# A decoder layer on one core: weights and remainders stored alternately, and requests moved in the front

## The chip, the cores and the metric

The kernel runs on one core of a Trainium2 chip. The core has TensorE (PE) for matmuls, VectorE (DVE), ScalarE (ACT) and GpSimd (POOL) for the rest, and SyncE (SP), which here issues nearly all transfers. The metric is the device time of one execution in microseconds (us); the timed runs of a kernel are compared by their median.

## The reference

One decoder layer for 256 tokens of width 1024, all in float32. Cut to what matters:

```
h = rmsnorm(x, norm_mix_g);  q, k, v, gu, gv, gate_a, gate_b = split(h @ w_in)
y_a = moba_attention(rope(q), rope(k), v) @ moba_w_proj        # 8 heads, one causal block of 256
y_b = gmlp_spatial_gating(gu, gv, ...) @ gmlp_w_proj
x = x + (sigmoid(gate_a) * y_a + sigmoid(gate_b) * y_b) @ w_out
x = x + memory_cross_attention(rmsnorm(x), rmsnorm(mem), xa_w_q, xa_w_kv, xa_w_o)
# PEER: 128 x 128 experts of one neuron, 8 heads, top 16
q = rmsnorm(x) @ peer_w_q;  s = q . subkeys                    # two scores per head and token
top 16 of s1, top 16 of s2, top 16 of their 256 sums -> experts e, g = softmax(top scores)
x = x + sum_k g_k * gelu(h . w_down[e_k]) * w_up[e_k]
return rmsnorm(x, final_g)
```

The kernel doesn't gather experts. It computes all 16384 of `h . w_down` (128 down blocks of 128 experts), multiplies by a gate that is zero where an expert wasn't chosen, and multiplies by all of `w_up` (128 up blocks).

## The kernel before

**Weights as a stream.** All weights lie in HBM as blocks of 128 x 1024 float32 (512 KB): 84 of the front (`wf`), 128 down (`wd`), 128 up (`wu`). `load_to` requests a block into one of four `raw` buffers on SP. `conv_to` splits it in two: ACT writes `hi`, the block rounded to fp32r (L140), and DVE the remainder `lw` = raw - hi (L142; for the routing's query blocks and the first five down blocks POOL does it). `take` hands a block to PE and first converts two blocks ahead (`LEAD`) and requests four more (`RAW`). Functions that were put into `later` run inside `take`, after that. Each product is then three fp32r matmuls: hi by hi, hi by remainder, remainder by hi (`mm3`, L179 to L181).

**Two kinds of blocks.** In most blocks the weights are the stationary operand: PE loads 128 columns of `hi` or `lw` and streams 256 columns of activations past them, 24 matmuls a block (`tblock` in the front, `down` for the experts, tile `A`). In 12 front blocks (`Natural`, indices 0 to 3, 12 to 15, 48, 49, 62, 63 of `wf`) and all up blocks (`umm`, tile `y`) the weights stream, 512 columns a matmul, past stationary activations: 12 matmuls a block. For up blocks the stationary operand is the gated activation, split into halves `gh` and `gl` in the tile `gahl`.

**Where the halves lie.** `hi` and `lw` are two tiles of three buffers each, every row contiguous. Small tiles `apart` and `rest` set their start 64 bytes behind a multiple of 512 (`APART`), and `GOFF` does the same for `gahl`.

**Order.** One program order, written out by hand; each engine runs its own instructions in it. Ahead: the first norm, q and k blocks with `rope`, attention, gates, gMLP, the memory's blocks, the output projection (`mp` by eight blocks, residual `x1T`, L606), cross-attention (`xquery`, `xscore`, `xscale`, `xtrans`, `xvalue`, with two value blocks `nm_.step()` among them), its projection, and 16 query blocks of the routing with the top-16 search of each (`best`) on DVE. Four remainders (`spread`) are already done in two halves of 512 there, popped from the list `half` at chosen places.

Then DVE merges the candidates (`work`, a list of pieces with an estimate of each), and `down` blocks are set beside it: `D0` = 22, one for each 1.55 us of estimate, and `D1` = 4 more while the last routing steps run. After them come 16 gate steps for the first 64 experts of each block (`gprep` on DVE makes one-hot fp16 patterns, `gstep` multiplies them on PE and ACT copies the result to `G`), then 64 up blocks, then 16 gate steps and 64 up blocks for the second half. `plan()` spreads the rest of the down blocks: a ring of 49 results (`RING`) bounds how many may be ahead, so the first gate stage has 49 - (D0 + D1 + 1) = 22 of them, the up stage 42, the second gate stage 22, the rest 15.

Of the kernel before, what the change touches and what calls it, by code (L numbers as in the profile page):

```python
# [16 lines left out]
F32 = mybir.dt.float32  # L17
# [10 lines left out]
S = 256  # L28
KD = 8
# [9 lines left out]
APART = 64  # L39
GOFF = (64, 64)  # L40
D0, D1 = 22, 4
# [4 lines left out]
N_XO, N_PQ = 4, 16  # L46
FIRST = 5
# [42 lines left out]
def body(tc, I, out, dbg=None):  # L90
# [18 lines left out]
    spread, half = range(nf - N_PQ - 2, nf - N_PQ + 2), []  # L109
    pos = {"load": 0, "conv": 0, "take": 0}  # L110

# [17 lines left out]
    def conv_to(n):  # L129
        while pos["conv"] < min(n, len(stream)):  # L130
            m = pos["conv"]
            load_to(m + 1)
            raw = raws.pop(m)
            hi = wst.tile([128, 1024], F32R, name="hi")
            lw = wst.tile([128, 1024], F32R, name="lw")
            parts = 2 if m in (1, 2) else 1
            halves = m in spread
            for p in range(parts):
                ps = slice(p * 1024 // parts, (p + 1) * 1024 // parts)
                A.copy(hi[:, ps], raw[:, ps])  # L140
                if not halves:
                    lo_engine(m).tensor_sub(lw[:, ps], raw[:, ps], hi[:, ps].bitcast(F32))  # L142
            if halves:
                for p in range(2):
                    ps = slice(p * 512, p * 512 + 512)
                    half.append(lambda ps=ps, lw=lw, raw=raw, hi=hi: V.tensor_sub(lw[:, ps], raw[:, ps],
                                                                                 hi[:, ps].bitcast(F32)))
            convs[m] = (hi, lw)
            pos["conv"] += 1
# [77 lines left out]
    P.dma_start(gcol, I["gcol"])  # L227
# [24 lines left out]
    class Squares:  # L252
# [5 lines left out]
        def add(self, src, sq=P, add=P):  # L258
            q = self.pool.tile([128, S], F32, name="sq", bufs=4)
            if sq is A:  # L260
                A.activation(q, src, AF.Square)
            else:
                sq.tensor_mul(q, src, src)
            if self.acc is None:
                self.acc = q
            else:
                add.tensor_add(q, q, self.acc)  # L267
                self.acc = q
# [20 lines left out]
    def tblock(w, x, n=KD, base=0):  # L289
        ps = pmm()  # L290
        for k in range(n):
            c = (base + k) * 128
            mm3(ps, w, (slice(None), slice(c, c + 128)), x, sl(k), k == 0, k == n - 1)
        return ps

    class Natural:
# [5 lines left out]
        def step(self):  # L302
            wh, wl = take("f")
# [17 lines left out]
    hi = wst.tile([128, 1024], F32R, name="hi")  # L321
    lw = wst.tile([128, 1024], F32R, name="lw")
# [23 lines left out]
    sqp.matmul()  # L346
# [6 lines left out]
    later.append(first_norm)  # L353
# [24 lines left out]
    for c in range(4):  # L378
        for nm in ("q", "k"):
            ps = tblock(take("f"), xg)  # L380
            if (c, nm) == (0, "q"):
                later.append(rope_norm)
# [221 lines left out]
    for c in range(KD):  # L604
        ps = tblock(take("f"), mp)
        V.tensor_add(x1T[:, c], ps, xT[:, c])  # L606
        split(xg1[0][:, c], xg1[1][:, c], x1T[:, c], gcol[:, 1, c:c + 1])
        pq.add(x1T[:, c], A, V)
    dump("x1T", x1T)
# [65 lines left out]
    xscale(1)  # L675
    xscore(3)
    xscale(2)
    nm_.step()
    xscale(3)
# [3 lines left out]
    P.dma_start(skh[0], I["skT"][:, 0:8])  # L683
    nm_.step()
    V.tensor_scalar(vm[:, 0], nm_.ps[0], rm[:, 0:1], None, op0=OP.mult)
    A.activation(vm[:, 1], nm_.ps[1], AF.Copy, scale=rm[:, 1:2])
    xtrans(0, 2)
# [63 lines left out]
    for n in range(16):  # L751
# [17 lines left out]
        if n == 7:  # L769
# [106 lines left out]
    for (us, fn) in work:  # L876
        fn()
        spent += us
        while n < D0 and spent > 1.55 * (n + 1) - 2.5:
# [115 lines left out]
    def up_b(i2):  # L995
        if i2 in GA:
            ga = GA.pop(i2)
            off = GOFF[i2 // QI] // 4
            gg_ = gp.tile([128, 2 * S + 128], F32R, name="gahl", bufs=4)
            gh, gl = gg_[:, off:off + S], gg_[:, off + S:off + 2 * S]  # L1000
# [169 lines left out]
```

## Time and profile before

| what | us |
|---|---|
| median of three timed runs (1053.73 to 1054.83) | 1054.41 |
| profiled execution, its own time | 1054.2 |
| its span, first to last instruction | 1052.2 |
| PE busy in the span | 1031.1 (98%) |
| DVE busy | 763.3 (73%) |
| ACT busy | 594.0 (56%) |
| POOL busy | 64.1 (6%) |

Times in rows are microseconds from the start of the span unless marked ns. A row of PE's timeline gives a matmul's start and its length in the pipeline; lengths overlap, so the pace is read from start to start. "PEld" are weight loads. A busy PE is not a PE at its peak.

### The profile page before, as it was taken

Reading aid. Unit: us, or ns where it says so; the run is one execution under the profiler, and the core shown is the slowest. Engines: PE = TensorE matmul, PEld = TensorE weight load, DVE = VectorE, ACT = ScalarE, POOL = GpSimd, SP = SyncE. Lnnn points to the kernel's source line nnn. Section 1 sums busy time; section 2 is a strip of 40 time slices with the busy share of each in tenths; the row PEclk is TensorE's granted clock in tenths of the full one; section 3 lists DMA queues with packets and bytes.
Section 4 is the critical chain, followed back from the end, with each engine's and each line's share of the span. In section 5 each row is a group of like instructions: output and inputs, shape, how many; then the busy total and the mean of one; then the engine's idle time right before and its main releaser. Section 6 shows DMA issues by size and latency. Waiting matters only on the chain.

```text
span 1052.2 us, 19738 instructions
## 1 busy us (share of the span) xinstructions
PE 1031.1 (98%) x7862; PEld 954.5 (91%) x7862; DVE 763.3 (73%) x1493; ACT 594.0 (56%) x935; POOL 64.1 (6%) x54
## 2 busy tenths in 40 slices
PE   8999999889999999999999999999999999999997
PEld 7989999889999999998889988999999988888886
DVE  6775797579999999965656565566799766666656
ACT  6865845457554557755454444444678644545454
POOL 0400000006650000000000000000000000000000
PEclk9999999899999999999999999999999999999999
DMA  8644655445446544465556655565544556566562
GB/s 283 235 138 128 200 170 174 134 152 170 151 158 202 166 140 152 134 187 189 192 187 194 191 190 189 191 195 188 160 147 154 176 189 196 187 195 191 191 197 103
DMA packets 52251, 185.83 MB, mean 177 GB/s; under 512 B 5808, under 2 KB 6720, under 8 KB 52032
## 3 DMA queue, kind: packets, MB, share of 16 engines
q1 hardware_dynamic: 51552, 183.20, 54.5%
q8 instruction: 61, 1.00, 0.4%
q0 software_dynamic: 320, 1.07, 0.3%
q10 hardware_dynamic: 288, 0.33, 0.1%
q14 instruction: 30, 0.25, 0.1%
HBM read 183.52 MB, written 1.05 MB: 175 GB/s over the span
## 4 chain that ended last, share of the span: by engine, by line
PE 85%; DVE 10%; ACT 3%; issue 1%; DMA 1%; SPq 0%; DVEq 0%; ACTq 0%
PE A L179 11%; PE y L1010 11%; PE y L1013 11%; PE y L1009 11%; PE A L181 11%; PE A L180 11%; PE mm L179 4%; PE mm L180 4%; PE mm L181 4%; DVE lw L142 2%; PE m L982 2%; ACT hi L140 2%; PE m L981 2%; DVE sq L267 1%; DVE X L727 1%
## 5 line engine op out<-in xcount | busy, mean ns | idle before, releaser
L142 DVE TENSOR_TENSOR lw<-raw,hi 128x1024 fp32r<-128x1024 f32 (+1 forms) x318 | 388.4, 1223 | 235.2 <-ACT hi L140 234.6
L140 ACT CAST hi<-raw 128x1024 fp32r<-128x1024 f32 (+1 forms) x341 | 355.2, 1043 | 191.0 <-issue 145.2
L179 PE MATMUL A<-mgh,hi 128*128 128x256 f32 x1024 | 290.6, 284 | 0.0
L181 PE MATMUL A<-mgh,lw 128*128 128x256 f32 x1024 | 288.0, 281 | 1.8 <-DVE lw L142 1.8
L180 PE MATMUL A<-mgl,hi 128*128 128x256 f32 x1024 | 287.8, 281 | 0.0
L181 PEld LDWEIGHTS A<-mgh,lw 128*128 128x128 f32 x1024 | 195.9, 191 | 2.2 <-DVE lw L142 2.2
L1010 PE MATMUL y<-lw,gahl 128*128 128x512 f32 x504 | 196.3, 390 | 0.0
L1009 PE MATMUL y<-hi,gahl 128*128 128x512 f32 x504 | 196.2, 389 | 0.0
L180 PEld LDWEIGHTS A<-mgl,hi 128*128 128x128 f32 x1024 | 192.9, 188 | 2.2
L179 PEld LDWEIGHTS A<-mgh,hi 128*128 128x128 f32 x1024 | 192.4, 188 | 2.2
L1013 PE MATMUL y<-hi,gahl 128*128 128x512 f32 x504 | 155.3, 389 | 0.0
L797 ACT ACTIVATE aring<-A 128x256 f32<-128x256 f32 x128 | 49.2, 384 | 161.4 <-PE A L181 161.4
L179 PE MATMUL mm<-xgh,hi 128*128 128x256 f32 x416 | 118.5, 285 | 0.2 <-DVE q L368 0.2
L181 PE MATMUL mm<-xgh,lw 128*128 128x256 f32 x416 | 116.2, 279 | 0.4 <-DVE lw L142 0.4
L180 PE MATMUL mm<-xgl,hi 128*128 128x256 f32 x416 | 116.0, 279 | 0.0
L1013 PEld LDWEIGHTS y<-hi,gahl 128*128 128x128 f32 x504 | 94.6, 188 | 19.6
L1010 PEld LDWEIGHTS y<-lw,gahl 128*128 128x128 f32 x504 | 94.7, 188 | 17.3
L1009 PEld LDWEIGHTS y<-hi,gahl 128*128 128x128 f32 x504 | 94.6, 188 | 17.4
L179 PEld LDWEIGHTS mm<-xgh,hi 128*128 128x128 f32 x416 | 78.3, 188 | 1.1 <-issue 0.7
L181 PEld LDWEIGHTS mm<-xgh,lw 128*128 128x128 f32 x416 | 78.6, 189 | 0.7 <-DVE lw L142 0.6
L180 PEld LDWEIGHTS mm<-xgl,hi 128*128 128x128 f32 x416 | 78.5, 189 | 0.0
L983 ACT ACTIVATE G<-m 128x512 f32<-128x512 f32 x64 | 65.9, 1140 | 5.0 <-PE m L982 2.3
(273 smaller groups left out, 1243.7 us busy)
## 6 DMA issues: line engine op xcount, KB each, us to landing
raw<-in_wd SPq DMA_DIRECT2D x128, 512.0 KB, 3.7
raw<-in_wu SPq DMA_DIRECT2D x128, 512.0 KB, 3.8
raw<-in_wf SPq DMA_DIRECT2D x83, 512.0 KB, 3.7
memT<-in_memT SPq DMA_DIRECT2D x1, 1024.0 KB, 7.8
xT<-in_xT SPq DMA_DIRECT2D x3, 256.0 KB, 7.0
out_y<-raw SPq DMA_DIRECT2D x3, 256.0 KB, 2.0
raw<-in_wf SPq DMA_DIRECT2D x2, 256.0 KB, 3.7
wmT<-in_wsT SPq DMA_DIRECT2D x1, 512.0 KB, 5.9
```

Source lines behind the costliest of these rows:

```text
L140: A.copy(hi[:, ps], raw[:, ps])
L142: lo_engine(m).tensor_sub(lw[:, ps], raw[:, ps], hi[:, ps].bitcast(F32))
L179: T.matmul(ps, wh[wsl], xh[xsl], start=start, stop=False)
L180: T.matmul(ps, wh[wsl], xl[xsl], start=False, stop=False)
L181: T.matmul(ps, wl[wsl], xh[xsl], start=False, stop=stop)
L797: A.activation(a, ps, AF.Gelu_apprx_tanh)
L981: T.matmul(ps[:, t], a1[at], bh[at], start=True, stop=False)
L982: T.matmul(ps[:, t], a1[at], bl[at], start=False, stop=True)
L983: A.activation(Gq[q][:, :, s * TG + c:s * TG + c + 8].rearrange("p i t -> p t i"), ps, AF.Copy, scale=1.0 / 16384.0)
L1009: T.matmul(yps[t][z], gh[:, tsl(t)], wh[:, zs], start=False, stop=False, skip_group_check=True)
L1010: T.matmul(yps[t][z], gh[:, tsl(t)], wl[:, zs], start=False, stop=False, skip_group_check=True)
L1013: T.matmul(yps[t][z], gl[:, tsl(t)], wh[:, zs], start=False, stop=False, skip_group_check=True)
```

## The change

Seven edits, in one diff (line numbers of the later kernel are some 15 higher from the top on):

- `hi` and `lw` become one tile `hl` of 2048. For blocks whose weights stream (`streamed`) its first half is `hi` and its second `lw` (`planar`); for all others, element by element, one of `hi` and one of `lw` (`woven`). `gahl` is woven too, without the offset, and `APART` is 128.
- `D0` is 26 and the pieces' pace 1.31 for 1.55. `plan()` then gives the first gate stage 49 - 31 = 18 down blocks, the up stage 46, the second gate stage 18, the rest 15.
- the mean square's matmuls move into the middle of the first q block, the broadcast of the norm into the middle of the first k block (`mid`); the norm itself is computed right behind the q block; `sq` has six buffers.
- the request of `gcol` goes from POOL to ACT.
- nine more remainders (`spread`) are done in halves: those of eight blocks in the output projection's loop and one behind `vm`.
- a value block goes ahead of `xscore(3)`, and `xscale(3)` behind a request.
- the third norm's broadcast goes one query block later.

```diff
-APART = 64
-GOFF = (64, 64)
-D0, D1 = 22, 4
+APART = 128
+D0, D1 = 26, 4
+NATURAL = [0, 1, 2, 3, 12, 13, 14, 15, 48, 49, 62, 63]
-    spread, half = range(nf - N_PQ - 2, nf - N_PQ + 2), []
+    spread, half = [*range(52, 60), nf - N_PQ - 3, *range(nf - N_PQ - 2, nf - N_PQ + 2)], []
+    def woven(x):
+        x = x.rearrange("p (c u) -> p c u", u=2)
+        return x[:, :, 0], x[:, :, 1]
+    def planar(x):
+        n = x.shape[1] // 2
+        return x[:, :n], x[:, n:]
+    def streamed(m):
+        kind, idx = stream[m]
+        return kind == "u" or kind == "f" and idx in NATURAL
-            hi = wst.tile([128, 1024], F32R, name="hi")
-            lw = wst.tile([128, 1024], F32R, name="lw")
+            hl = wst.tile([128, 2048], F32R, name="hl")
+            hi, lw = planar(hl) if streamed(m) else woven(hl)
-    P.dma_start(gcol, I["gcol"])
+    A.dma_start(gcol, I["gcol"])
-            q = self.pool.tile([128, S], F32, name="sq", bufs=4)
+            q = self.pool.tile([128, S], F32, name="sq", bufs=6)
-    def tblock(w, x, n=KD, base=0):
+    def tblock(w, x, n=KD, base=0, mid=None):
         ps = pmm()
         for k in range(n):
+            if mid and k == n // 2:
+                mid()
...
     nv.step()
-    sqp.matmul()
...
-            ps = tblock(take("f"), xg)
-            if (c, nm) == (0, "q"):
-                later.append(rope_norm)
+            first = c == 0
+            ps = tblock(take("f"), xg, mid=(sqp.matmul if nm == "q" else rope_norm) if first else None)
+            if first and nm == "q":
+                first_norm()
...
         V.tensor_add(x1T[:, c], ps, xT[:, c])
+        half.pop(0)()
         split(xg1[0][:, c], xg1[1][:, c], x1T[:, c], gcol[:, 1, c:c + 1])
         pq.add(x1T[:, c], A, V)
+        half.pop(0)()
...
     xscale(1)
+    nm_.step()
     xscore(3)
     xscale(2)
-    nm_.step()
-    xscale(3)
     xtrans(0, 0)
     xtrans(1, 0)
...
+    xscale(3)
     nm_.step()
     V.tensor_scalar(vm[:, 0], nm_.ps[0], rm[:, 0:1], None, op0=OP.mult)
     A.activation(vm[:, 1], nm_.ps[1], AF.Copy, scale=rm[:, 1:2])
+    for _ in range(2):
+        half.pop(0)()
...
-        if n == 7:
+        if n == 8:
             bcast(r3, r3bc)
...
-        while n < D0 and spent > 1.55 * (n + 1) - 2.5:
+        while n < D0 and spent > 1.31 * (n + 1) - 2.5:
...
-            off = GOFF[i2 // QI] // 4
-            gg_ = gp.tile([128, 2 * S + 128], F32R, name="gahl", bufs=4)
-            gh, gl = gg_[:, off:off + S], gg_[:, off + S:off + 2 * S]
+            gh, gl = woven(gp.tile([128, 2 * S], F32R, name="gahl", bufs=4))
```

On DVE, at the end of the output projection's loop, the order before is this (`lw` the remainder of a block two ahead, `xT` the residual sum, `xg1l` the remainder of the next operand, `sq` the squares' sum):

```order
L142 TENSOR_TENSOR lw<-raw,hi 128x1024
L606 TENSOR_TENSOR xT<-mm,xT 128x256
L175 SCALAR_TENSOR_TENSOR xg1l<-xT,gcol,xg1h 128x256
L267 TENSOR_TENSOR sq<-sq 128x256
L142 TENSOR_TENSOR lw<-raw,hi 128x1024 x2
```

And of the change, at the same place (`hl<-raw,hl` is a half of a remainder; the last row are the whole ones of the next two blocks):

```order
L621 TENSOR_TENSOR xT<-mm,xT 128x256
L160 TENSOR_TENSOR hl<-raw,hl 128x512
L189 SCALAR_TENSOR_TENSOR xg1l<-xT,gcol,xg1h 128x256
L281 TENSOR_TENSOR sq<-sq 128x256
L160 TENSOR_TENSOR hl<-raw,hl 128x512
L156 TENSOR_TENSOR hl<-raw,hl 128x1024 x2
```

The residual sum of a block now stands ahead of a remainder, and the remainder is cut in two around the next operand's split.

On DVE in cross-attention, before (`Px` the softmax's numerators, `xr` a reciprocal, `PT` a copy of transposes, `vm` the memory's values):

```order
L142 TENSOR_TENSOR lw<-raw,hi 128x1024
L649 RECIPROCAL xr<-xs 128x2
L651 TENSOR_SCALAR Px_2414<-Px_2414,xr 128x256
L651 TENSOR_SCALAR Px_2415<-Px_2415,xr 128x256
L641 COPY PT<-at 128x512
L142 TENSOR_TENSOR lw<-raw,hi 128x1024
L685 TENSOR_SCALAR vm<-nat_1749,rrr 128x512
```

Of the change:

```order
L658 COPY PT<-at 128x512
L666 RECIPROCAL xr<-xs 128x2
L668 TENSOR_SCALAR Px_2362<-Px_2362,xr 128x256
L668 TENSOR_SCALAR Px_2363<-Px_2363,xr 128x256
L702 TENSOR_SCALAR vm<-nat_1707,rrr 128x512
L160 TENSOR_TENSOR hl<-raw,hl 128x512 x2
```

The remainder that stood ahead of `vm` stands behind it, in halves.

On PE, at the end of the fourth query block, before (`at<-kT,qT` the scores of two heads, `nat` a value block):

```order
L181 MATMUL mm<-xg1h,lw 128x256
L625 MATMUL at<-kT,qT 128x256 x4
L310 MATMUL nat_1749<-hi,mgh 128x512
L311 MATMUL nat_1749<-lw,mgh 128x512
L312 MATMUL nat_1749<-hi,mgl 128x512
```

Of the change, from the last matmul of the value block on (the third head's two stand ahead of its 12 matmuls):

```order
L329 MATMUL nat_1708<-hl,mgl 128x512
L642 MATMUL at<-kT,qT 128x256 x2
L655 MATMUL at<-ident,Px_2362 128x128 x4
L655 MATMUL at<-ident,Px_2363 128x128 x4
L327 MATMUL nat_1707<-hl,mgh 128x512
```

The value block lies between the scores of the third and the fourth head, where the two stood in a row.

## Rows read from the trace of the kernel before

**Rows 1.** Part 4 of the page: the chain that ended last, by engine.

```profile
PE 85%; DVE 10%; ACT 3%; issue 1%; DMA 1%; SPq 0%; DVEq 0%; ACTq 0%
```

**Rows 2.** Stages: length, each engine's busy us (instructions), granted clock, DMA share, GB/s.

```profile
192.00:204.00 12.00, 9.67 (x52) 9.23 (x52) 7.41 (x17) 5.04 (x10) 0.00 (x0) 0.72 0.56 171
238.00:293.70 55.70, 53.99 (x461) 53.60 (x460) 53.26 (x260) 35.06 (x69) 38.81 (x16) 1.00 0.50 161
293.70:374.40 80.70, 78.56 (x666) 77.91 (x664) 77.33 (x313) 40.08 (x59) 11.08 (x14) 1.00 0.55 178
374.40:453.80 79.40, 79.36 (x1042) 78.34 (x1042) 71.93 (x85) 59.63 (x75) 0.00 (x0) 1.00 0.44 140
453.80:746.70 292.90, 292.90 (x1779) 263.02 (x1779) 176.37 (x238) 142.37 (x213) 0.00 (x0) 1.00 0.60 191
746.70:829.00 82.30, 82.27 (x1066) 81.22 (x1065) 74.17 (x89) 62.54 (x80) 0.00 (x0) 1.00 0.46 145
829.00:1045.00 216.00, 216.00 (x1127) 186.20 (x1126) 138.10 (x210) 107.85 (x164) 0.00 (x0) 1.00 0.58 184
```

**Rows 3.** Timeline of PE, 102 to 105 us: start, length, line, operation, tiles.

```profile
102.50 0.28 PE L179 MATMUL mm<-xgh,hi 128*128 128x256 f32 x1
...
105.22 0.28 PE L179 MATMUL mm<-xgh,hi 128*128 128x256 f32 x1
```

**Rows 4.** Timeline of PE, 699 to 705 us.

```profile
699.68 0.28 PE L179 MATMUL A<-mgh,hi 128*128 128x256 f32 x1
...
702.51 0.39 PE L1009 MATMUL y<-hi,gahl 128*128 128x512 f32 x1
...
705.23 0.28 PE L179 MATMUL A<-mgh,hi 128*128 128x256 f32 x1
```

**Rows 5.** Timeline of PE, 377 to 378 us: one gate step.

```profile
377.20 0.20 PE L981 MATMUL m<-bh,a 128*128 128x64 f16 x1
...
378.19 0.36 PE L179 MATMUL A<-mgh,hi 128*128 128x256 f32 x1
```

**Rows 6.** Timeline of PE ahead of 224 us; in brackets the wait before.

```profile
20.66 0.61 PE L273 MATMUL at<-ones,sq 128*128 128x1 f32 x4 [0.98 <-DVE sq L267]
...
169.01 0.28 PE L179 MATMUL mm<-xgh,hi 128*128 128x256 f32 x1
...
196.66 0.39 PE L179 MATMUL mm<-xg1h,hi 128*128 128x256 f32 x1 [1.82 <-ACT xg1h L170]
...
204.48 0.47 PE L179 MATMUL mm<-xg1h,hi 128*128 128x256 f32 x1
...
213.88 1.13 PE L625 MATMUL at<-kT,qT 128*128 128x256 f32 x4 [1.76 <-ACT qT L620]
...
223.81 1.38 PE L658 MATMUL mm<-PT,vm 128*128 128x128 f32 x10 [1.52 <-DVE vm L685]
```

**Rows 7.** Timeline of DVE and ACT, 194 to 196 us.

```profile
194.51 1.23 DVE L142 TENSOR_TENSOR lw<-raw,hi 128x1024 fp32r<-128x1024 f32 x1 [0.42 <-ACT hi L140]
...
195.65 0.42 DVE L606 TENSOR_TENSOR xT<-mm,xT 128x256 f32<-128x256 f32 x1
...
196.10 0.51 ACT L170 ACTIVATE xg1h<-xT,gcol 128x256 fp32r<-128x256 f32 x1 [1.63 <-DVE xT L606]
```

**Rows 8.** Groups of DVE by form: line, count, busy us, mean ns.

```profile
L142 DVE TENSOR_TENSOR lw<-raw,hi 128x1024 fp32r<-128x1024 f32 x314 | 385.9, 1230 | 234.7 <-ACT hi L140 234.1
...
L146 DVE TENSOR_TENSOR lw<-raw,hi 128x512 fp32r<-128x512 f32 x8 | 5.5, 686 | 0.4
```

**Rows 9.** Groups of ACT by form.

```profile
L983 ACT ACTIVATE G<-m 128x512 f32<-128x512 f32 x64 | 65.9, 1140 | 5.0 <-PE m L982 2.3
...
L643 ACT COPY PT<-at 128x512 f32<-128x512 f32 x2 | 1.2, 582 | 0.0
```

**Rows 10.** Groups of DVE by form, 328 to 361 us.

```profile
L844 DVE SCALAR_TENSOR_TENSOR jk<-XP,CE 128x48 f32<-128x48 f32 x4 | 0.8, 211 | 0.0
...
L844 DVE SCALAR_TENSOR_TENSOR jk<-XP,CE 128x32 f32<-128x32 f32 x4 | 0.8, 201 | 0.0
```

More of the change, by code (lines that the diff above doesn't have):

```diff
@@ L302, in step @@
         def step(self):
+            assert streamed(pos["take"])
             wh, wl = take("f")
@@ L320, in body @@
     wst.tile([128, APART // 4], F32, name="apart", bufs=1)
-    hi = wst.tile([128, 1024], F32R, name="hi")
-    lw = wst.tile([128, 1024], F32R, name="lw")
+    hi, lw = planar(wst.tile([128, 2048], F32R, name="hl"))
     wst.tile([128, 128 - APART // 4], F32, name="rest", bufs=1)
@@ L351, in first_norm @@
         r1 = rms_nat(sqp, fp, "r1")
-    later.append(first_norm)
     rbc = fp.tile([128, S], F32, name="rbc")
```

## Prediction

> **What bounds the kernel now.** I read the chain of waits first, because it says which engine set the end: TensorE (PE) holds 85% of it, VectorE (DVE) 10% [rows 1]. Next the busy times by stage [rows 2]. From 453.8 to 746.7 us and from 829 to 1045 us PE is busy without a gap, so there the time is matmuls times pitch (start to start) and nothing else. From 238 to 374.4 us, the routing, DVE is busy 53.26 of 55.7 and 77.33 of 80.7 us beside a PE almost as full. In the two stages that spread the gates (374.4 to 453.8 and 746.7 to 829) PE is full and DVE has 7.5 and 8.1 us of air. Only ahead of 224 us does PE stand, and from 192 to 204 us its granted clock is 0.72, so partly at 1.2 GHz; inside that stretch it had stood 1.82 us at 196.66 [rows 6].
>
> Then the pitch itself. The same three matmuls over the same shapes run at two levels: 24 of them take 2.72 us at 102.50 (113.3 ns each) [rows 3] and 2.83 us at 699.68 (117.9 ns) [rows 4], both at full clock (1.00 in that stage, rows 2). 256 columns at 2.4 GHz are 106.7 ns, so 6.7 or 11.2 ns lie on top. An up block, 12 matmuls of 512 columns, takes 2.72 us (702.51 to 705.23): 226.7 ns, 13.3 above its columns. Every matmul has its own weight load, beside the matmul before it (x1779 of each in the up stage, rows 2). What differs between the levels is how the load and the running matmul meet in memory, since clock, shape and engine are alike. The change alters just that: where the loaded weights lie.
>
> A rule of the Trainium skill speaks against this. "TensorE: Matmul & The Clock Gate" (Part 2, step 1, LDWEIGHTS) says that TensorE has two independent read ports, so that loading the next weights takes nothing from the running matmul. By it the layout changes no pitch, which is rival A. The trace disagrees so far as 113.3 and 117.9 ns stand there for one form.
>
> **The change part by part.** The time is made against the profiled execution, 1054.2 us (span 1052.2); the median of the timed runs, 1054.41, is the same within 0.2.
>
> *Alternating.* Stationary weights and their remainders now lie at every second place. A load of 128 then walks 1024 bytes in the time in which a 256-column matmul walks 1024, so the two can keep one distance instead of crossing. Three prices are unknown. (a) The pitch. Best case: the gate matmuls read alternate fp16 places on both sides and need 0.99 us for 32 of 64 columns [rows 5], 30.9 ns against 26.7, so 4.3 on top; a block would be 2.66 us and an up block 2.61. Worst side: a load that walks twice as far is slower than now; each ns costs about 2 us, as 91 blocks of 24 matmuls lie in the stages where PE rules (30, 46 and 15). I take 113.3 ns, the faster level that the same form already shows, thus 2.72 us a block; the up blocks I leave at 226.7, because their excess is the same 1/16 of the columns that the 113.3 has, which looks like a cost of the moving operand. (b) ScalarE's and DVE's writes at every second place. ScalarE's gate copy, which scatters each element, takes 1140 ns for 512 where a plain one takes 582 [rows 9], so the upper end is a doubling. DVE's runs of two elements take 201 ns for 32, its runs of three 211 for 48 [rows 10]: nothing on top. Two per stretch is what the change makes, so I take zero. (c) The smaller tile of gate halves and the new base offset: no instruction, zero.
>
> *Front, ahead of 169 us.* The mean-square matmuls move into the middle of the first q block, so PE's 0.98 us for them at 20.66 [rows 6] goes: -1.0. The gcol request goes from GpSimd's queue to ScalarE's, where one ident request waits behind it; I count zero, as the stream of x behind it is what comes late next. The front's blocks run mostly at the fast level; zero.
>
> *Remainders in halves, 169 to 204 us.* In each block of the output projection DVE's remainder of 1.23 us stands ahead of the residual sum: it starts at 194.51, the sum at 195.65, and ScalarE's first half of the next operand at 196.10 [rows 7]. That ring of ScalarE and DVE, not PE, sets the pace, and PE ends up standing. Now the sum comes first and two halves of 686 ns [rows 8] lie behind it. DVE's work per block is then 0.42 + 0.69 + 0.48 + 0.42 + 0.69 = 2.7 us (the sum 0.42 in rows 7; the split and the squares I put at 0.48 and 0.42 like it), level with a PE block of 2.72. From 169.01 to 204.48 [rows 6] ten blocks run: 10 x 2.72 plus some 1.4 for two small groups (0.61 for four such at 20.66) is 28.6 instead of 35.5: -6.9. The halves themselves cost 8 x 0.14 on DVE, beside PE.
>
> *Requests moved, 204 to 224 us.* PE stands 1.76 us ahead of the scores at 213.88 and 1.52 at 223.81 for vm, where a remainder was ahead of it on DVE [rows 6]. A value step of 12 matmuls now lies before the last scores, and vm is ahead of the remainder. The softmax on ScalarE and DVE is late next, so I take half: -1.6. Bounds for the whole front: 0 to -11.2 (all waits).
>
> *Mean square broadcast one block later, 238 to 293.7 us.* DVE rules; zero.
>
> *Four more blocks beside the routing.* Four of 26 blocks move from each gate stage's 22 or 23 (which get 18 or 19) to the routing (30) and to the up stage (46 instead of 42). Each carries a 1.22 us remainder on DVE. Routing: PE 78.56 + 4 x 2.83 - 30 x 0.11 = 86.6, DVE 77.33 + 4.9 = 82.2; PE rules, +5.9 against 80.7. First gate stage: PE 79.4 - 11.3 - 18 x 0.11 = 66.1, DVE 71.93 - 4.9 = 67.0 and some 2 us for its waits on ScalarE, so DVE rules: 69, -10.4. Up stage: 46 x 2.72 - 42 x 2.83 = +6.3. Second gate stage: DVE 74.17 - 4.9 and 1.2 = 70.5 against PE 68.9: -11.8. Last stage, 15 blocks: -1.7.
>
> Sum: -1.0 - 6.9 - 1.6 + 5.9 - 10.4 + 6.3 - 11.8 - 1.7 = -21.2, so **1033 us**.
>
> **The rivals.** *A, the pitch stays at 117.9.* For it: the slower level holds through all of the late stages, and a load over twice the bytes may meet the matmul as often. Against: the 113.3. Then routing +9.2, gate stages -10.4 and -11.3, up stage +11.3, last stage 0, front -9.5: -10.7, **1043.5**. Moving blocks then only exchanges PE time between stages, and the front is the gain.
>
> *B, both pitches fall to 4.3 ns above their columns.* For it: rows 5, where loads and matmuls both read alternate places. Against: those are fp16 and short, and the up blocks show the same 226.7 throughout. Front -9.5, routing 84.8 (+4.1), gate stages -10.4 and -11.8 (DVE), up stage 46 x 2.66 - 42 x 2.83 - 64 x 0.11 = -3.5, last stage -15 x 0.17 - 62 x 0.11 = -9.4: -40.5, about **1014**.
>
> *C, slower: DVE's remainder at every second place takes longer.* Its place is the routing and the gate stages, where DVE has no air left: 30 + 18 + 19 remainders. From the forecast's sums, e us more for each costs 67e less the 4.4 that DVE has free in the routing; the 21.2 are gone at e = 0.38, when 1.22 becomes 1.6. At a doubling (e = 1.2) it is 1054.2 - 21.2 + 76, some **1109 us**. For it: rows 9 on ScalarE. Against: rows 10 on DVE itself.
>
> **How the numbers follow.** Chances: forecast 0.40, A 0.20, B 0.20, C 0.20. A measurement of this kernel tells 0.2%, 2.1 us, from no change. Forecast and B are faster by more; of A 0.17 is, and 0.03 falls within if the front gives back little; of C 0.17 is slower and 0.03 within. So faster 0.77, same 0.06, slower 0.17. The range 1006 to 1058 holds forecast, A, most of B and the mild end of C; some 0.05 lies below and 0.15 above. The forecast's own range is 1025 to 1042 (front 0 to -11, gate stages +-3).
>
> **What the new profile would show.** Right: 24 matmuls of a down block in 2.72 us in the up stage and 12 of an up block still in 2.72; DVE's remainder still 1.22 us and ScalarE's first half no longer than now; the granted clock 1.00 between 190 and 200 us; gate stages of 69 to 71 us in which DVE is busier than PE's share would ask. Down blocks of 2.83 show A, up blocks near 2.6 show B, a remainder above 1.6 shows C. The forecast is wrong in the front if PE still stands over 1 us ahead of the first query block or ahead of the last scores.

## The result and the profile after

The changed kernel takes 1090.87 us (median of 4 runs, 1090.79 to 1092.01) against 1054.62 for the kernel before on the same chip: ratio 1.0346, 95% interval 1.0328 to 1.0364, 36 us slower where 21 faster was predicted. The profiled execution has a span of 1090.3 us. Its chain of waits holds less of PE and more of DVE than in [rows 1]:

```profile
PE 79%; DVE 15%; ACT 2%; issue 2%; DMA 1%; SPq 0%; DVEq 0%; ACTq 0%
```

The busy times by stage, cut at the first query block, the first down block of the routing, and the first gate matmul and first up block of each half ([rows 2] has some of its cuts up to 3 us earlier; the table of stages below cuts both kernels alike). A row gives stretch, length, then PE, PEld, DVE, ACT, POOL, granted clock, DMA share, GB/s:

```profile
192.00:204.00 12.00, 12.00 (x99) 11.90 (x98) 9.81 (x23) 6.92 (x12) 0.00 (x0) 1.00 0.67 220
...
239.30:309.30 70.00, 56.28 (x457) 54.92 (x455) 67.25 (x254) 34.71 (x67) 38.96 (x16) 0.97 0.41 133
309.30:406.70 97.40, 95.81 (x785) 95.33 (x785) 87.20 (x325) 48.56 (x67) 11.19 (x13) 0.99 0.52 165
406.70:478.50 71.80, 71.01 (x946) 69.39 (x945) 66.69 (x82) 58.19 (x70) 0.00 (x0) 1.00 0.40 130
478.50:790.10 311.60, 311.60 (x1875) 283.96 (x1874) 179.91 (x240) 152.16 (x218) 0.00 (x0) 1.00 0.58 187
790.10:861.90 71.80, 71.01 (x946) 69.38 (x945) 67.21 (x82) 58.10 (x70) 0.00 (x0) 1.00 0.41 130
861.90:1082.90 221.00, 221.00 (x1129) 193.63 (x1128) 138.32 (x210) 110.36 (x164) 0.00 (x0) 1.00 0.56 180
```

Two things stand out. The query blocks take 70.0 us where they took 55.1, and there PE is busy for only 56 of them: it waits. And the up stages, where PE still never waits, are longer at the same full clock: the matmuls themselves come more slowly. PE's timeline of one down block (24 matmuls) and one up block (12), answering to [rows 4]:

```profile
518.06 0.28 PE L193 MATMUL A<-mgh,hl 128*128 128x256 f32 x1
...
520.97 0.40 PE L1026 MATMUL y<-hl,gahl 128*128 128x512 f32 x1
...
523.76 0.28 PE L193 MATMUL A<-mgh,hl 128*128 128x256 f32 x1
```

2.91 and 2.79 us, thus 121.1 and 232.3 ns a matmul, where 113.3 and 226.7 were forecast and 117.9 and 226.7 stood before. PE's longest waits in the query blocks (us in total, times, longest), and a group of DVE in the same stretch (count, busy us, mean ns, idle before):

```profile
PE at L766 <- ACT qp L781: 12.2, 6, 4.4
```

```profile
L187 DVE TENSOR_TENSOR mgl<-hx,mgh 128x256 fp32r<-128x256 f32 x7 | 15.5, 2232 | 0.0
```

Six waits of PE, up to 4.4 us, on the copy of a query block. And the seven `mgl` splits of 256 columns take 2.23 us on average, nearly twice as long as a remainder of 1024 columns (1230 ns): six take some 2.5 us, and one that runs beside no instruction of POOL 0.41 us. In the timeline of DVE, POOL and ACT of one query block:

```profile
283.73 2.43 POOL L156 TENSOR_TENSOR hl<-raw,hl 128x1024 fp32r<-128x1024 f32 x1 [3.12 <-ACT hl L154]
283.89 2.55 DVE L187 TENSOR_TENSOR mgl<-hx,mgh 128x256 fp32r<-128x256 f32 x1
...
286.36 0.47 DVE L756 SCALAR_TENSOR_TENSOR hx<-x2T,gcol,r3bc 128x256 f32<-128x256 f32 x1
...
286.87 0.42 ACT L184 ACTIVATE mgh<-hx 128x256 fp32r<-128x256 f32 x1 [3.22 <-DVE hx L756]
...
287.19 0.35 ACT L781 COPY qp<-mm 128x256 f32<-128x256 f32 x1
...
287.71 1.16 ACT L154 CAST hl<-raw 128x1024 fp32r<-128x1024 f32 x1
...
288.94 2.43 POOL L156 TENSOR_TENSOR hl<-raw,hl 128x1024 fp32r<-128x1024 f32 x1 [2.79 <-ACT hl L154]
289.11 2.55 DVE L187 TENSOR_TENSOR mgl<-hx,mgh 128x256 fp32r<-128x256 f32 x1
```

`mgl` begins 0.16 us after POOL's remainder and ends 0.28 us after it (283.73 + 2.43 = 286.16). Behind it stand `hx`, ACT's `mgh`, its copy `qp`, its cast, and then POOL's next remainder, beside which the next `mgl` starts: a ring of 5.2 us a block. In the kernel before a block took 3.2 to 3.3 us, and `mgl` (535 ns on average) came when POOL was nearly done. The same wait can be read there:

```profile
278.26 2.40 POOL L142 TENSOR_TENSOR lw<-raw,hi 128x1024 fp32r<-128x1024 f32 x1 [0.79 <-ACT hi L140]
...
280.42 0.52 DVE L173 TENSOR_TENSOR mgl<-hx,mgh 128x256 fp32r<-128x256 f32 x1
```

POOL ends at 280.66, `mgl` at 280.94, 0.28 us later, and so do six of the eight splits of the kernel before (0.52 to 0.62 us long); the one beside no instruction of POOL takes 0.41 us. The Trainium skill ("SBUF — State Buffer", section "Who interferes with whom") says that DVE and GpSimd share one pair of ports, and that it is an exclusive lock. These rows agree: the split does not end before POOL has.

Elsewhere the front did what was forecast: PE is busy 12.00 of 12.00 us at full clock where [rows 2] had 9.67 at 0.72 (at the same times; the blocks there start some 5 us later than before), and the four waits of [rows 6] are gone; what is left of PE's waits between 200 and 239 us is 0.9, 0.4 and 0.2 us. DVE's remainder is unchanged, ACT's cast and gate copy hardly longer (these over the whole span, answering to [rows 8] and [rows 9]):

```profile
L156 DVE TENSOR_TENSOR hl<-raw,hl 128x1024 fp32r<-128x1024 f32 x305 | 374.8, 1230 | 254.0 <-ACT hl L154 253.2
```

```profile
L154 ACT CAST hl<-raw 128x1024 fp32r<-128x1024 f32 x337 | 371.6, 1103 | 193.0 <-issue 147.9 <-PE y L1030 28.3 <-PE mm L195 10.6
L1002 ACT ACTIVATE G<-m 128x512 f32<-128x512 f32 x64 | 66.6, 1151 | 9.0 <-PE m L1001 8.0
```

### The profile page after: what moved, and what is told of

Same layout as the page of the kernel before. It is cut to its first block, busy times and chain, and to the rows that moved or that the text cites. A ratio compares the mean times of both kernels' runs of the same rounds, so it can differ in the third digit from the quotient of the medians.

```text
span 1090.3 us, 19742 instructions
## 1 busy us (share of the span) xinstructions
PE 1062.0 (97%) x7862; PEld 987.5 (91%) x7862; DVE 780.9 (72%) x1502; ACT 614.4 (56%) x935; POOL 63.8 (6%) x53
## 4 chain that ended last, share of the span: by engine, by line
PE 79%; DVE 15%; ACT 2%; issue 2%; DMA 1%; SPq 0%; DVEq 0%; ACTq 0%
PE y L1027 11%; PE y L1026 11%; PE y L1030 11%; PE A L193 9%; PE A L195 9%; PE A L194 9%; PE mm L193 5%; PE mm L195 5%; PE mm L194 5%; DVE hl L156 3%; DVE a L969 2%; DVE bl L984 2%; DVE mgl L187 1%; DVE a L975 1%; ACT hl L154 1%
## 5 line engine op out<-in xcount | busy, mean ns | idle before, releaser
L156 DVE TENSOR_TENSOR hl<-raw,hl 128x1024 fp32r<-128x1024 f32 (+1 forms) x309 | 377.4, 1223 | 254.8 <-ACT hl L154 254.0
L154 ACT CAST hl<-raw 128x1024 fp32r<-128x1024 f32 (+1 forms) x341 | 373.9, 1098 | 193.7 <-issue 147.9
L193 PE MATMUL A<-mgh,hl 128*128 128x256 f32 x1024 | 295.0, 288 | 0.0
L195 PE MATMUL A<-mgh,hl 128*128 128x256 f32 x1024 | 291.0, 284 | 1.3 <-DVE hl L156 1.3
L194 PE MATMUL A<-mgl,hl 128*128 128x256 f32 x1024 | 291.0, 284 | 0.0
L194 PEld LDWEIGHTS A<-mgl,hl 128*128 128x128 f32 x1024 | 201.2, 197 | 2.4
L193 PEld LDWEIGHTS A<-mgh,hl 128*128 128x128 f32 x1024 | 200.3, 196 | 2.2
L195 PEld LDWEIGHTS A<-mgh,hl 128*128 128x128 f32 x1024 | 200.5, 196 | 1.5 <-DVE hl L156 1.5
L1026 PE MATMUL y<-hl,gahl 128*128 128x512 f32 x504 | 198.7, 394 | 0.0
L1027 PE MATMUL y<-hl,gahl 128*128 128x512 f32 x504 | 198.3, 394 | 0.0
L1030 PE MATMUL y<-hl,gahl 128*128 128x512 f32 x504 | 157.5, 394 | 0.0
L193 PE MATMUL mm<-xgh,hl 128*128 128x256 f32 x416 | 120.6, 290 | 0.4 <-DVE q L382 0.4
L195 PE MATMUL mm<-xgh,hl 128*128 128x256 f32 x416 | 118.1, 284 | 0.0
L1030 PEld LDWEIGHTS y<-hl,gahl 128*128 128x128 f32 x504 | 98.4, 195 | 17.9
L1027 PEld LDWEIGHTS y<-hl,gahl 128*128 128x128 f32 x504 | 99.0, 196 | 15.8
L1026 PEld LDWEIGHTS y<-hl,gahl 128*128 128x128 f32 x504 | 98.8, 196 | 15.9
L193 PEld LDWEIGHTS mm<-xgh,hl 128*128 128x128 f32 x416 | 81.2, 195 | 1.3 <-issue 0.7
L195 PEld LDWEIGHTS mm<-xgh,hl 128*128 128x128 f32 x416 | 80.8, 194 | 0.0
L1002 ACT ACTIVATE G<-m 128x512 f32<-128x512 f32 x64 | 66.6, 1151 | 9.0 <-PE m L1001 8.0
```

What stands on the lines that cost most here:

```text
L193: T.matmul(ps, wh[wsl], xh[xsl], start=start, stop=False)
L194: T.matmul(ps, wh[wsl], xl[xsl], start=False, stop=False)
L195: T.matmul(ps, wl[wsl], xh[xsl], start=False, stop=stop)
L1002: A.activation(Gq[q][:, :, s * TG + c:s * TG + c + 8].rearrange("p i t -> p t i"), ps, AF.Copy, scale=1.0 / 16384.0)
L1026: T.matmul(yps[t][z], gh[:, tsl(t)], wh[:, zs], start=False, stop=False, skip_group_check=True)
L1027: T.matmul(yps[t][z], gh[:, tsl(t)], wl[:, zs], start=False, stop=False, skip_group_check=True)
```

## The experiments

Lengths of stages (us) in the profiles that the experiments are read by, each from its first instruction to that of the next stage, the last one to the last up matmul (the cut ahead of the query blocks lies 0.2 to 0.3 us behind their first matmul, in every row alike):

| kernel | to the first query block | query blocks | routing | gates 1 | up | gates 2 | rest of up | span |
|---|---|---|---|---|---|---|---|---|
| before | 238.7 | 55.1 | 83.5 | 79.5 | 292.8 | 79.3 | 216.3 | 1052.2 |
| after | 239.3 | 70.0 | 97.4 | 71.8 | 311.6 | 71.8 | 221.0 | 1090.3 |
| e1 | 229.9 | 56.3 | 91.7 | 71.3 | 304.1 | 71.3 | 216.3 | 1048.3 |
| e2 | 244.9 | 56.1 | 85.4 | 81.3 | 300.0 | 81.3 | 221.0 | 1077.2 |
| e3 | 237.8 | 58.1 | 96.5 | 71.9 | 311.6 | 71.9 | 221.0 | 1076.0 |
| e4 | 235.5 | 66.6 | 85.3 | 79.3 | 292.8 | 79.4 | 216.3 | 1062.3 |
| e11 | 230.3 | 53.9 | 82.6 | 79.1 | 292.8 | 79.5 | 216.3 | 1041.8 |
| e13 | 231.2 | 53.9 | 91.5 | 71.3 | 304.1 | 70.9 | 216.3 | 1046.5 |

### Which part costs what: e1 to e4

**e1**, from the changed kernel:

```diff
-APART = 128
+APART = 64
-            hi, lw = planar(hl) if streamed(m) else woven(hl)
+            hi = wst.tile([128, 1024], F32R, name="hi")
+            lw = wst.tile([128, 1024], F32R, name="lw")
-            gh, gl = woven(gp.tile([128, 2 * S], ...))
+            gg_ = gp.tile([128, 2 * S + 128], ...)
+            gh, gl = gg_[:, 16:16 + S], gg_[:, 16 + S:16 + 2 * S]
```

> The changed kernel with hi and lw of the weights, and the gate halves, stored one behind the other again at the old base offset; every other part of the change stays. Theory 1 (the alternating storage costs pitch, and the later broadcast costs the query blocks their rhythm, two separate losses): down blocks back near 118 ns and up blocks at 226.7 ns a matmul, the query-block stage still near 71 us with VectorE's mgl split near 2.0 us; total 1054.6 - 9 (front) - 1.2 (exchange of blocks at 117.9 ns, as in rival A) + 15.6 = about 1060 us. Theory 2 (the alternating storage causes both, the query blocks because ScalarE's first half and the matmuls take longer): query-block stage near 56 us, total about 1044 us, as rival A.

Measured: 1063.74 us, ratio 1.0064 (1.0023 to 1.0105), but in two groups of runs, three at 1049.3 to 1051.4 us and seven at 1062.2 to 1065.6. The profile is of the first: query blocks 56.3 us, pitches as before. Neither theory foresaw both groups. The pitch goes back with the storage and its offsets, which this edit undoes together. With storage in a row and the late broadcast the total falls either way from run to run; that the query blocks make the difference is likely from its size (13 us), but not shown, as the slower group has no profile.

**e2**, from the kernel before: the edit of e1 the other way round.

> The kernel before with the alternating weights and gate halves alone (base offset 128 with them). Theory 1 (pitch and broadcast are separate losses): query-block stage near 57 us; down blocks near 121 ns, up blocks near 231 ns a matmul; total 1054.6 + some 150 blocks x 24 x 3.5 ns (12.6) + 128 x 12 x 4.5 ns (6.9) = about 1074 us. Theory 2 (the storage causes both): the query-block stage too goes to about 71 us, total about 1090 us.

Measured: 1079.93 us (ratio 1.0244, 1.0200 to 1.0289), query blocks 56.1 us, down and up blocks as in the changed kernel. The storage, with the offsets that go with it, costs 26.7 us and does not tip the query blocks.

**e3**, from the changed kernel (**e4** is the opposite edit in the kernel before):

```diff
-        if n == 8:
+        if n == 7:
             bcast(r3, r3bc)
```

> The changed kernel with the mean-square broadcast back beside query block 7 instead of 8, nothing else undone. If the broadcast's place tips the query blocks (theory 1): mgl split back near 0.54 us, the stage near 57 us, total about 1090.9 - 15 = 1076 us. If the storage does it (theory 2): mgl stays near 2.0 us and the total near 1091 us.

> The kernel before with nothing but the mean-square broadcast moved beside query block 8. Theory 1: the mgl split goes to about 2 us, the query-block stage from 55.7 to about 71 us, total about 1070 us. Theory 2, and the prediction (which put this move at zero): 1054.5 us.

Measured: e3 1077.22 us, 13.7 below the changed kernel; e4 1065.12 (ratio 1.0106, 1.0063 to 1.0150), 11.9 above the kernel before. In e4 the splits take as long as in the changed kernel:

```profile
L173 DVE TENSOR_TENSOR mgl<-hx,mgh 128x256 fp32r<-128x256 f32 x7 | 14.8, 2128 | 0.0
```

So theory 1 holds: two separate losses, though e4's is smaller than its forecast (1065 us for 1070). What I had put at zero, a broadcast moved by one block, costs 12 to 14 us.

### Why the query blocks tip: e7 and e9

**e7**, from e4:

```diff
-        later.append(lambda: split(h3[0][:, k], h3[1][:, k], hx))
+        later.append(lambda: split(h3[0][:, k], h3[1][:, k], hx, eng=P))
```

> The kernel before with the broadcast beside query block 8 (which alone took 1065 us) and the eight mgl splits on GpSimd, behind its remainder in its own queue, instead of on VectorE. If the loss is VectorE's two-operand mgl standing until GpSimd's remainder ends: VectorE has no instruction of over 1.5 us in the query blocks, the stage is back to about 55 us, total about 1053 us. If the loss is the late broadcast itself (work pushed behind the last query blocks): the stage stays near 66 us, total about 1065 us.

Measured: one run of 1050.95 us and four of 1062.2 to 1063.6; the profile is of the one. There `hx`, DVE's other instruction on two operands, has taken up the wait (930 ns against 474 in the kernel before). By itself this settles nothing.

**e9**, from e4:

```diff
-                    lo_engine(m).tensor_sub(lw[:, ps], ...)
+                    e = lo_engine(m)
+                    for qs in [slice(z * 256, z * 256 + 256) for z in range(4)] if e is P else [ps]:
+                        e.tensor_sub(lw[:, qs], ...)
```

> The kernel before with the broadcast beside query block 8 (1065 us) and GpSimd's remainder of a block issued as four quarters of 256 columns instead of one instruction of 2.43 us. Theory 1 (a two-operand instruction of VectorE stands until the GpSimd instruction that runs beside it has ended): no mgl or hx above some 1.2 us, stage 55 to 58 us, total 1053 to 1057 us. Theory 2 (the late broadcast itself puts work behind the query blocks; GpSimd has no part): stage near 66 us, total about 1065 us.

Measured: 1055.13 us, runs from 1052.6 to 1056.9 in one group, ratio 1.0002 (0.9987 to 1.0017), though the broadcast is as late as in e4. Query blocks 55.7 us; DVE and POOL in that stretch:

```profile
L739 DVE SCALAR_TENSOR_TENSOR hx<-x2T,gcol,r3bc 128x256 f32<-128x256 f32 x8 | 6.9, 874 | 0.1
...
L175 DVE TENSOR_TENSOR mgl<-hx,mgh 128x256 fp32r<-128x256 f32 x7 | 4.7, 678 | 0.0
```

```profile
L144 POOL TENSOR_TENSOR lw<-raw,hi 128x256 fp32r<-128x256 f32 x64 | 48.6, 793 | 17.2 <-ACT hi L140 17.0
```

The same work of POOL in shorter instructions, and the loss of 10 us is gone, while POOL's own time grew from 38.6 to 48.6 us. Theory 1, shown: DVE stands for the rest of the POOL instruction beside which it starts. A lengthened `mgl` or `hx` of e4 ends 0.28 us after POOL's whole remainder, one of e9 0.28 us after a quarter, and none in e9 takes over 0.96 us. In the profiles of all these kernels together, 171 `mgl` and `hx` start while an instruction of POOL runs; 166 of them end 0.28 us or more after it, and the other five start within 0.03 us of POOL's start. The late broadcast only sets when it starts.

### What raises the pitch: e5, e6, e10, e12, e14 to e18

**e5** and **e6**, both from e3; e6 stores all halves one behind the other (`planar` for `woven`), and the diff is e5's, without the indexing that follows from it:

```diff
-        x = x.rearrange("p (c u) -> p c u", u=2)
+        x = x.rearrange("p (k u w) -> p k u w", u=2, w=128)
```

> The changed kernel with the broadcast at query block 7 and hi and lw (and the gate halves) alternating in runs of 128 elements instead of 1: the same tiles at the same addresses, but each load of 128 weights reads neighbours. If the step inside one load costs the pitch: weight loads back from 196 to 188 ns, down blocks near 117 ns, up blocks 226.7 ns a matmul, total about 1077 - 27 = 1050 us. If it is the nearness of hi and lw, or the base offset, that costs: pitches stay at 120.9 and 231.6 ns, total 1077 us.

> The changed kernel with the broadcast at query block 7, all halves one behind the other, at the base offset of the changed kernel (128, no extra offset for the gate halves) instead of 64. If the two levels of the pitch (113 and 118 ns) come from the base offset, the down blocks stand at one of the two alone: at 113.3 the total is about 1050 - 128 x 24 x 3.5 ns = 1039 us, at 118 about 1055 us. If the offset has no say: mean 116.5 ns as with offset 64, 1050 us.

**e10**, from the kernel before, and **e12**, from e3 (gate halves at 64 with it):

```diff
-APART = 64
+APART = 128
```

```diff
-APART = 128
+APART = 64
```

> The kernel before with nothing but the base offset of the weights' tiles, 64 bytes to 128 (the gate halves stay at 64). If the offset of the weights costs, as the run with all halves in a row at 128 suggests: down blocks near 118.7 ns and the front's near 118.8; total 1054 + 128 x 24 x 2.2 ns (6.8) + 70 x 24 x 3.8 ns (6.4) = about 1067 us if the up blocks stay at 226.7 (their excess then comes from the gate halves' offset), about 1075 us if they go to 232 with the weights' offset alone. If the offset of weights has no say: 1054 us.

> The changed kernel with the broadcast at query block 7 (1077 us) and its alternating tiles, weights and gate halves, begun at 64 bytes instead of 128 and 0. If step inside a load and offset each cost by themselves (2 ns and 2.2 to 5.6 ns): down blocks near 118.5 ns, up blocks near 226.7 ns, total about 1077 - 17 = 1060 us. If the offset matters only for halves in a row: 120.9 and 231.6 ns stay, 1077 us.

**e14**, from the kernel before; **e15** is the same with `APART = 128`:

```diff
+    mid.tile([128, 16], F32, name="mapart")
     mg = pair("mg", mid)
+    mid.tile([128, 112], F32, name="mrest")
```

> The kernel before with the moving operand of the down blocks (mgh, mgl) begun at 64 bytes instead of 0; the weights stay at 64. If the place of the weights relative to the moving operand sets the pitch (64 apart is good): both now stand alike and the down blocks go to about 119 ns, total 1054 + 128 x 24 x 2 ns = 1060 us. If the weights' own place counts: 116 to 118 ns, 1054 us. Up blocks 226.7 in both.

> The same with the weights at 128: moving operand and weights are 64 apart again, the other way round. Relative place: down blocks 116 to 118 ns, total 1066.4 - 6 = about 1060 us (the front's blocks and the up blocks stay as in the run with offset 128). Weights' own place: 119 ns, 1066 us.

**e16**, from the kernel before:

```diff
-            gh, gl = gg_[:, off:off + S], gg_[:, off + S:off + 2 * S]
+            gg_ = gg_[:, off:off + 2 * S].rearrange("p (c u) -> p c u", u=2)
+            gh, gl = gg_[:, :, 0], gg_[:, :, 1]
```

> The kernel before with the gate halves alone alternating, at their old offset of 64 bytes; weights in a row at 64. If the alternating stationary operand costs whatever its offset: up blocks about 233 ns, down blocks 116 to 118 ns, total 1054 + 128 x 12 x 6.5 ns = 1064 us. If up blocks lose only by the weights (moving operand) having moved: 226.7 ns, 1054 us.

All of them together, with one down and one up block of the up stage read from start to start as above, and the base offsets that the program gives weights, down blocks' moving operand, and gate halves, in bytes:

| kernel | storage | weights, moving, gates | down, up block us | total us |
|---|---|---|---|---|
| before | in a row | 64, 0, 64 | 2.83, 2.72 | 1054.6 |
| after | alternating | 128, 0, 0 | 2.91, 2.79 | 1090.9 |
| e5 | runs of 128 | 128, 0, 0 | 2.88, 2.80 | 1068.3 |
| e6 | in a row | 128, 0, 0 | 2.85, 2.78 | 1067.6 |
| e10 | in a row | 128, 0, 64 | 2.88, 2.76 | 1066.4 |
| e12 | alternating | 64, 0, 64 | 2.88, 2.80 | 1076.4 |
| e14 | in a row | 64, 64, 64 | 2.87, 2.75 | 1061.2 |
| e15 | in a row | 128, 64, 64 | 2.75, 2.75 | 1055.1 |
| e16 | gates alternating | 64, 0, 64 | 2.73, 2.79 | 1059.6 |
| e17 | in a row | 128, 64, 128 | 2.83, 2.72 | 1045.9 |
| e18 | in a row | 128, 64, 64 | 2.83, 2.77 | 1048.9 |

First, the step inside a load: e5 and e6 end alike and 9 us below e3, and their loads take 189 and 188 ns where alternating ones take 196 (weight loads of down blocks between 500 and 700 us; the changed kernel, then e6):

```profile
L193 PEld LDWEIGHTS A<-mgh,hl 128*128 128x128 f32 x238 | 46.7, 196 | 1.1
```

```profile
L193 PEld LDWEIGHTS A<-mgh,hl 128*128 128x128 f32 x239 | 45.0, 188 | 1.2
```

Neither total is one that its forecast named (1050 or 1077 us for e5; 1039, 1050 or 1055 for e6). e6 has no alternating halves left and is still 13 us above the kernel before (ratio 1.0130, 1.0109 to 1.0151), with up blocks at 2.78 us. e16 reaches the same from the other side: the gate halves alternate, nothing else changes, and an up block takes 2.79 us.

```profile
513.71 0.28 PE L179 MATMUL A<-mgh,hi 128*128 128x256 f32 x1
...
516.44 0.39 PE L1010 MATMUL y<-hi,gahl 128*128 128x512 f32 x1
...
519.23 0.28 PE L179 MATMUL A<-mgh,hi 128*128 128x256 f32 x1
```

Its total is 5.0 us above the kernel before and not 10 as forecast, as its down blocks fall to 2.73 us.

Second, the offset, in which I had seen no cost: e10 changes nothing else and is 11.2 us slower (ratio 1.0101, 1.0079 to 1.0122).

```profile
502.74 0.28 PE L179 MATMUL A<-mgh,hi 128*128 128x256 f32 x1
...
505.62 0.40 PE L1009 MATMUL y<-hi,gahl 128*128 128x512 f32 x1
...
508.38 0.28 PE L179 MATMUL A<-mgh,hi 128*128 128x256 f32 x1
```

e12 shows that the two do not add: alternating storage at 64 is no better than at 128 (1076.4 against 1077.2 us, where 1060 was forecast if they did). Third, e14 spoils the down blocks by moving the other operand alone, and e15, with both moved, has them faster than the kernel before (e14, then e15):

```profile
500.15 0.28 PE L179 MATMUL A<-mgh,hi 128*128 128x256 f32 x1
...
503.02 0.40 PE L1011 MATMUL y<-hi,gahl 128*128 128x512 f32 x1
```

```profile
500.65 0.28 PE L179 MATMUL A<-mgh,hi 128*128 128x256 f32 x1
...
503.39 0.39 PE L1011 MATMUL y<-hi,gahl 128*128 128x512 f32 x1
```

2.87 us in e14, 2.74 in e15. (The expectation of e15 calls its distance the other way round; 128 against 64 lies the same way round as 64 against 0 in the kernel before.) So the place of the weights against the moving operand counts: storage in a row at the distances of the kernel before is a good case, and both a shift and alternating storage leave it. It is not all that counts: e15's down blocks have the distance of the kernel before and take 2.75 for 2.83 us, e6 and e10 are alike in weights and moving operand and stand at 2.85 and 2.88, and e14's up blocks rise to 2.75 though neither of their operands was moved.

**e17** is e11 (below) with `APART = 128` and the first line of e14 (`mapart`) without the second, so that all that lies behind it moves by 64; in **e18** the gate halves are moved back by 64.

> The front edits with GpSimd's quarters (1045.5 us), weights at 128 and everything stored behind them (moving operands, gate halves) 64 bytes on, so that all distances are those of that kernel. If distance alone sets the pitch: down blocks at 113.3 or 117.8 ns in a mix as there (mean 116.5), up blocks 226.7, total 1045 us within 2. If the places as such make the lower level (as in the run with moving operand at 64 and weights at 128, 114.1 ns): down blocks near 114 ns, total about 1045 - 128 x 24 x 2.4 ns = 1038 us.

> The same with the gate halves 64 bytes nearer (at 64, weights at 128), the distances of the run that showed 114.1 ns. If the up blocks before a down block decide which of its two levels it takes: down blocks near 114.1 ns and up blocks near 229 ns, total about 1045 - 7.4 + 128 x 12 x 2.3 ns (3.5) = 1041 us. If not: down blocks as in the other run and up blocks 229 ns, 1049 us.

e17 keeps every distance and equals e11 (1045.91 against 1045.51, with the same down and up blocks): moving everything alike costs nothing. e18 comes out as the second of its two cases (1048.91 us): its down blocks stay at 2.83, though its three offsets are those of e15 and its up blocks, at 2.77, are slower. And within one profile at one set of addresses both levels occur: in the routing of e11 nearly all blocks take 113.3 ns a matmul, in its up stage all 117.8. What picks the level at a good distance stays open; that it is the phase in which load and matmul follow each other is a guess.

### The front and the blocks: e8, e11, e13

**e8**: the changed kernel with e1's and e3's edits and `D0, D1 = 22, 4` with the old pace 1.55. **e11** adds the quarters of e9, **e13** to that:

```diff
-D0, D1 = 22, 4
+D0, D1 = 26, 4
-        while n < D0 and spent > 1.55 * (n + 1) - 2.5:
+        while n < D0 and spent > 1.31 * (n + 1) - 2.5:
```

> The kernel before with the edits of the front alone (mean square inside the first q block, gcol request, halves of remainders, value block and vm moved, six squares): storage, blocks beside the routing and the broadcast as before. By the first query block's start in the run without alternating storage (229.9 us against 238.7): total 1053.5 - 8.8 = about 1044.7 us. By the prediction's -9.5 for the front: 1044. If the front's gain is given back by the wait on the routing: near 1053 us.

> The front edits alone (1048.3 us, runs from 1045.0 to 1048.9) with GpSimd's remainders in quarters. If the spread of those runs and 1 to 3 us of the query blocks come from VectorE standing beside GpSimd: the query blocks near 55 us and the total 1044 to 1046 us with less spread. If GpSimd's shorter instructions only cost overhead: 1048 us or more.

> The front edits with GpSimd's quarters (1045.5 us) and in addition the four more blocks beside the routing. Prediction's terms for the exchange with the pitch left at 117.9 ns (rival A): +9.2 - 10.4 + 11.3 - 11.3 = -1.2, total about 1044 us. By the run without alternating storage, where the same stages stood at +8.2 - 8.2 + 11.3 - 8.0 against the kernel before: +3.3, total about 1049 us.

Measured: e8 1048.31 us (ratio 0.9941, 0.9923 to 0.9959; 1044 to 1045 was forecast): the first query block starts 9.7 us earlier in its profile (229.0 against 238.7), and some of that is lost in the query blocks (56.4). e11 1045.51 (ratio 0.9907, 0.9889 to 0.9926), query blocks 53.9: the best version of this study, 9.7 us faster than the kernel before. e13 1051.26 (ratio 0.9955, 0.9939 to 0.9972): the exchange of blocks costs 5.8 us between the medians, 4.7 between the profiled runs, where rival A's terms gave -1.2.

## Why the prediction was wrong

**Alternating, (a).** The step that failed first. It read the two levels of [rows 3] and [rows 4] as set by where the weights lie, and took the faster one for the new layout. Measured: 121.1 and 232.3 ns for 113.3 and 226.7. With the prediction's own counts, 46 x 2.91 + 64 x 2.79 = 312.4 us for the up stage, against 311.6 measured and 299.2 forecast. The worst side stood in the text ("a load that walks twice as far is slower than now"), but no rival carried it, and the up blocks were held at 226.7 by a remark on 1/16 of the columns that e16 refutes (2.79 us by the gate halves' storage alone). With the old offsets instead of the new ones the alternating storage costs as much (e12), so it is the layout that the step had wrong, and not its base alone. And the trace of before could have told me: within its first gate stage, from the same tiles, blocks of the faster level stand among others at 117.8 ns, so that addresses alone do not pick the level. One of them, from its first matmul to the gate matmul behind its 24:

```profile
403.61 0.28 PE L179 MATMUL A<-mgh,hi 128*128 128x256 f32 x1
...
406.33 0.20 PE L981 MATMUL m<-bh,a 128*128 128x64 f16 x1
```

That is 2.72 us, 113.3 ns a matmul.

**Alternating, (c).** "The smaller tile of gate halves and the new base offset: no instruction, zero." It holds no instruction, but e10 puts 11.2 us on the weights' offset alone.

**Alternating, (b).** Zero was right, and rival C is out: DVE's remainder stays 1230 ns; ACT's cast goes from 1048 to 1103. C had the sign by another mechanism.

**Rival A and the rule behind it.** Both pitches rose, so A is out too. The Trainium skill's two independent read ports ("TensorE: Matmul & The Clock Gate", Part 2, step 1) would leave both pitches untouched by layout; e10 and e14 show pitches that move with a distance between loads and moving operand, and there the measurement decides.

**Mean square broadcast one block later: "DVE rules; zero".** The second failed step, 12 to 14 us. That DVE was busy 53.26 of 55.7 us [rows 2] was the very reason not to write zero: its busy time does not say what else can stop it. POOL's 38.81 us stood in the same row, and the splits that end 0.28 us after POOL's remainder stood in the same trace.

**Four more blocks beside the routing.** With the pitch as before, the profiles of e13 and e11 show +8.9, -7.8, +11.3, -8.6 and 0, thus +3.8, against rival A's +9.2, -10.4, +11.3, -11.3, 0. The stages that rule by PE were right to 0.3 us; the gate stages gave 5 us less. I had let DVE rule them, but with 18 blocks PE is busy 69.36 of 71.3 us there and DVE 66.74 (e13, first gate stage).

**Front.** -9.5 forecast for the start of the query blocks; 9.7 in e8 and 8.8 in e1. The matmuls that start at 169.01, 204.48 and 238.43 in the kernel before start at 167.14, 195.60 and 228.79 in e8. So the halves of remainders gave 7.0 for 6.9, while the other two terms gave 1.9 for 1.0 and 0.8 for 1.6: that these two sum up right is luck. In the changed kernel all of the gain is eaten by the pitch: the first query block starts at 239.3 (238.7 before).

Sum by parts, in totals: front -5.9 (e8), blocks +5.8 (e13 against e11), broadcast +13.7 (e3), storage and offset +26.7 (e2), together +40 against 36 measured, so they overlap by some 4 us.

## What to carry to other kernels

Where TensorE is full, the place of stationary against moving operand can be a cost of its own, here 7 to 11 us for 64 bytes (e14, e10): change one offset at a time and read the pitch from start to start, in more than one stage. Where GpSimd and VectorE work side by side, look for two-operand VectorE instructions whose length jumps to that of the GpSimd one beside them, and cut GpSimd's work into shorter instructions before moving anything else. A step that is moved past a full engine is not free because it has no instruction of its own.

## What was not expected of the hardware

- A shift of all weights by 64 bytes: 2.83 to 2.88 us a down block, 2.72 to 2.76 an up block (e10).
- A matmul level that one set of addresses does not fix: 113.3 and 117.8 ns in one profile (e11). Down blocks fall to 2.73 us in e16, where the up blocks ahead of them are slower, but not in e18, where they are slower too.
- An instruction of VectorE on two operands of 256 columns that starts while one of GpSimd runs ends no earlier than 0.28 us after it (166 of 171 cases): `mgl` takes 0.41 us alone and up to 2.55 beside a remainder.
- One program in two courses: e1's runs fall into 1049 to 1051 and 1062 to 1066 us, and e7's into 1051 and 1062 to 1064.
